# Correction products of a three-product projection on bfloat16 operands instead of float32r

## The chip, the cores and the metric

The kernel runs on one core of a Trainium2 chip. The metric is the device time of one execution, in microseconds (us); the median of the runs shown counts. TensorE (PE) multiplies; PEld is its loading of the stationary operand (the weights of a matmul); VectorE (DVE), ScalarE (ACT) and GpSimd (POOL) work on tiles elementwise; SyncE (SP) issues the DMAs.

## The reference

A decoder trunk of two layers on 1024 tokens of width 1024, in float32. Cut to what matters:

```
for layer in (0, 1):
    h = x @ w_in[layer]                       # [main | mem q | main gate | mem gate]
    y_main = pool(u_main)                     # layer 0: trailing means, windows 2, 4, 8, 16, then a 256x256 map per group
             forgetting_attention(u_main)     # layer 1: 16 heads of 64, keys/values/forget gates = x @ w_kv_shared
    y_mem = memory_attention(q_mem, mem)      # 4 heads of 128 into 256 memory tokens, mkv = mem @ w_mem_kv
    y = concat(y_main * silu(g_main), y_mem * silu(g_mem)) @ w_out[layer]
    x = layer_norm(alpha * x + y)
```

## The kernel before, in words

**Three products for one.** A float32 operand is split into a high part, its rounding to float32r, and a low part, what is left. A product of two such operands is computed as three matmuls into one PSUM bank: high by high, high by low, low by high. All three take float32r operands. `hi_lo` (lines 138 to 142) makes the parts: ACT rounds (line 141), DVE subtracts (line 142). During layer 1's attention the weights are split by `gp_hi_lo` (lines 144 to 146), both operations on POOL; the flag `low` selects it in `split_w` (line 148).

**Slabs.** `slab` (from line 170) computes 128 output columns of a projection for all 1024 tokens: two weight pieces of 4 x 128 rows (`split_w`: a DMA into a `raw` buffer, then the split into `w` tiles, of which there are six, that is three pairs), two PSUM banks of 512 tokens, and for each of 4 row blocks in a piece the three matmuls one behind the other (line 184). One slab is 48 matmuls of 512 columns. Query, key, value, gate and pooling inputs are all slabs, 62 of them.

**The other users of split operands.** `mem_kv` projects the memory tokens (line 218, 256 columns); `probs` in `mem_attention` and the pooling map use `mm3` (line 168); `v_first` (line 622, 272 columns) computes the first values and the forget logits; `OutProj.products` (line 401) the output projection, 12 matmuls for each of 4 banks and each third of the rows. The attention's own logits (also `mm3`, line 168) use keys and queries whose halves are stacked, two float32r matmuls, and are not touched; probabilities by values (line 796) are f16.

**What sets the order.** At the start the x tiles come one by one (`load_x`), and the first two slabs' matmuls are put in order by a scheduler as their inputs come. In the memory attention and in layer 1's attention (`fox`) TensorE's order is written out: `Fill.pump` takes slab matmuls, counted in columns, between the attention's own. The transposes that turn the normed rows of layer 0 into layer 1's input are popped one at a time (`spread`) between projection matmuls. On POOL, layer 1's attention also needs the causal masks (line 736, one for each head and row block, each waiting for DVE's reading of the block before), and the gate products (lines 823 and 833).

**Buffers.** The x stream has two tiles under tag `A` (high and low, 32 KB a partition each); the weights, memory keys, queries and output rows have a pair of tiles each under their tags.

Of the kernel before, what the change touches and what calls it, by code (L numbers as in the profile page):

```python
# [18 lines left out]
P = 128  # L19
# [6 lines left out]
MH = 4  # L26
# [46 lines left out]
def trunk_kernel(ctx, tc, x, xT, memT, win, wk, wv0, wv, wmk, wmv, wout, poolw, pscale, lng, lnb, bforget, out):  # L73
# [42 lines left out]
    def wt(shape):  # L116
        return sb(list(shape), "w", 6, F32R)
# [4 lines left out]
    def w_slots(tags, where):  # L122

        def tiles(k):
            tag, bufs = tags[k]
            if tag == "w":
                return [[wt([P, NH]) for _ in range(2)] for _ in range(2)]
            if tag == "MK":
                pair = [MK([P, 2, NH]) for _ in range(2)]
            elif tag == "PG":  # L130
                pair = [sb([P, 2, NH], "P", 4, F32R), sb([P, 2, NH], "G", 4, F32R)]
            else:
                pair = [sb([P, 2, NH], tag, bufs, F32R, where) for _ in range(2)]
            return [[t[:, j, :] for j in range(2)] for t in pair]

        return tiles

    def hi_lo(hi, lo, src, pinned=False):

        pin = tc.keep_in_program_order if pinned else lambda ins: ins  # L140
        pin(nc.scalar.copy(hi, src))  # L141
        pin(nc.vector.tensor_tensor(lo, src, hi.bitcast(F32), ALU.subtract))  # L142

    def gp_hi_lo(hi, lo, src):
        nc.gpsimd.tensor_scalar(hi, src, 1.0, 1.0, ALU.mult, ALU.mult)  # L145
        nc.gpsimd.tensor_tensor(lo, src, hi.bitcast(F32), ALU.subtract)  # L146

    def split_w(src_dram, shape):
        r = raw(shape)
        nc.sync.dma_start(r, src_dram)  # L150
        h, l = wt(shape), wt(shape)
        (gp_hi_lo if low[0] else hi_lo)(h, l, r)
        return h, l
# [16 lines left out]
    def slab(pieces_dram, XH, XL, evac, banks=("pj", 2)):  # L170
# [4 lines left out]
        for n, pc in ((0, 0), (1, 0), (0, 1), (1, 1)) if arrived else ((0, 0), (0, 1), (1, 0), (1, 1)):  # L175
# [23 lines left out]
    def mem_kv(l):  # L199

        mh = [T([P, 4, NMEM]) for _ in range(2)]
        ml = [T([P, 4, NMEM]) for _ in range(2)]
        for q in range(4):
            r = raw([P, 2, NMEM])
            nc.sync.dma_start(r, memT[:, 2 * q : 2 * q + 2, :])
            hi_lo(mh[q // 2][:, 2 * (q % 2) : 2 * (q % 2) + 2, :], ml[q // 2][:, 2 * (q % 2) : 2 * (q % 2) + 2, :], r)
        kh, kl = MK([P, MH, NMEM]), MK([P, MH, NMEM])

        def project(w_dram):

            acc = ps([P, NH], "pj", 2)[:, :NMEM]
            for pc in range(2):
                a, b = split_w(w_dram[pc], [P, 4, P])
                for k in range(4):
                    if k % 2:
                        spread()
                    for i, (w, m) in enumerate(((a, mh), (a, ml), (b, mh))):
                        nc.tensor.matmul(  # L218
                            acc, w[:, k, :], m[pc][:, k, :],
                            start=pc == 0 and k == 0 and i == 0, stop=pc == 1 and k == 3 and i == 2,  # L220
                        )
            return acc
# [4 lines left out]
        def keys(h):  # L227
            hi_lo(kh[:, h, :], kl[:, h, :], project(wmk[l, h]))
# [9 lines left out]
        return (kh, kl, v, undo), keys, vals  # L238
# [18 lines left out]
    def transposes(src, n, dst_h, dst_l):  # L257

        def one(g, j):
# [3 lines left out]
            if j == 3:  # L263
                hi_lo(dst_h(g), dst_l(g), banks[g])
# [9 lines left out]
    def gate_units(w_dram, dst, XH, XL):  # L274
        return slab(w_dram, XH, XL, lambda cols, acc: gate(acc, dst[:, cols]))

    def mem_attention(l, XH, XL, kv, qtile, ytile, yd):

        (kh, kl, v, undo), keys, vals = kv
# [4 lines left out]
        for h in range(MH):  # L284
            while turns:
                spread()
            qh, ql = qtile(), qtile()
            run(slab(win[l, 8 + h], XH, XL, lambda cols, acc: hi_lo(qh[:, cols], ql[:, cols], acc)))
            qs.append((qh, ql))
# [5 lines left out]
        for h in range(MH):  # L295
            fill.add(gate_units(win[l, 20 + h], gs[h], XH, XL), SLAB)

        def probs(i):
# [3 lines left out]
            for hp in range(2):  # L302
                lg = ps([P, 2, NMEM], "L", 3)
                for j in range(2):
                    h = 2 * hp + j
                    qh, ql = (t[:, i * P : (i + 1) * P] for t in qs[h])
                    mm3(lg[:, j, :], ((qh, kh[:, h, :]), (qh, kl[:, h, :]), (ql, kh[:, h, :])))
# [46 lines left out]
    class OutProj:  # L354
# [23 lines left out]
        def split(self, upto, pinned=False):  # L378

            while self.n < upto:  # L380
# [5 lines left out]
                h, lo = self.ws[nh][kk]  # L386
                hi_lo(h[j], lo[j], self.raws.pop(0), pinned)
# [6 lines left out]
        def products(self, accs, c, yh, yl):  # L394
            for a in range(2):
                for nh in range(2):
                    for k in range(4):
                        kt = 4 * c + k
                        wh, wl = (w[kt % 2] for w in self.ws[nh][kt // 2])
                        for i, (y, w) in enumerate(((yh, wh), (yh, wl), (yl, wh))):  # L400
                            nc.tensor.matmul(  # L401
                                accs[a][nh], y[:, k, a * P : (a + 1) * P], w,
                                start=kt == 8 and i == 0, stop=kt == 7 and i == 2,
# [3 lines left out]
        def early(self, y, yh, yl):  # L407
# [4 lines left out]
            for two in (slice(0, 2), slice(2, 4)):  # L412
                hi_lo(yh[:, two, :], yl[:, two, :], y[:, two, :], True)
                yield
            self.accs = self.open()
            yield from self.products(self.accs, 2, yh, yl)

        def rest(self, resid, XH, XL, dst):
# [11 lines left out]
            for sp, c in order + [(sp, c) for sp in range(2, ST // 2) for c in (2, 0, 1)]:  # L430
                if c == 2:
                    accs[sp] = self.open((("T", 2), ("T", 2), ("L", 3), ("O", 1))) if 0 in accs and sp == 1 else self.open()
                src, yh, yl = T([P, 4, 2 * P], F32), T([P, 4, 2 * P]), T([P, 4, 2 * P])
                nc.sync.dma_start(src, self.yd[c, :, :, sp * 2 * P : (sp + 1) * 2 * P])
                hi_lo(yh, yl, src)
                for k, _ in enumerate(self.products(accs[sp], c, yh, yl)):
                    if c != 2 and k % 6 == 5:
                        spread()
                if c == 1:
                    norm(sp, accs.pop(sp), gb, resid, XH, XL, dst)  # L440

    def norm(sp, accs, gb, resid, XH, XL, dst):
        for a in range(2):
# [22 lines left out]
            if XH is not None:  # L466
                transposes(
                    z, KT,
                    lambda g, rows=rows: XH[:, 4 * g : 4 * g + 4, rows],
                    lambda g, rows=rows: XL[:, 4 * g : 4 * g + 4, rows],  # L470
                )


    XH, XL = (sb([P, KT, S], "A", 2, F32R) for _ in range(2))

    def load_x(kt, parts=1):
        r = T(dt=F32)
        for i in range(parts):
            cols = slice(i * S // parts, (i + 1) * S // parts)
            nc.sync.dma_start(r[:, cols], xT[kt, :, cols])  # L480
            hi_lo(XH[:, kt, cols], XL[:, kt, cols], r[:, cols])
# [17 lines left out]
    with tc.tile_pool(name="in0", bufs=1) as in0:  # L499

        def bt():
            return sb([P, S], "B", 8, F32R, in0)

        def pool_group(g):
            w = WINDOWS[g]
            pms = []
            for f in (2 * g, 2 * g + 1):
                u = sb([P, S], "P", 4)
                run(slab(
                    first[f] if g == 0 else win[0, f], XH, XL, lambda cols, acc: nc.scalar.copy(u[:, cols], acc),  # L510
# [12 lines left out]
                ph, pl = T(), T()  # L523
                hi_lo(ph, pl, pm)
                pms.append((ph, pl))
            r = raw([P, 2, 2 * P])
            nc.sync.dma_start(r, poolw[g])
            wh, wl = (MK([P, 2, 2 * P]) for _ in range(2))
            hi_lo(wh, wl, r)
            ys = []  # L530
            for f in (2 * g, 2 * g + 1):
                y = sb([P, S], "Y", 4, F32, in0)
                run(gate_units(win[0, 12 + f], y, XH, XL))
                ys.append(y)
            for d in range(2):
                f = 2 * g + d
                for n in range(2):
                    acc = ps([P, NH], "L", 3)
                    terms = []
                    for ct in range(2):  # L540
                        a, b = wh[:, ct, d * P : (d + 1) * P], wl[:, ct, d * P : (d + 1) * P]
                        ph, pl = (t[:, n * NH : (n + 1) * NH] for t in pms[ct])
                        terms += [(a, ph), (a, pl), (b, ph)]
# [9 lines left out]
        mem_attention(0, XH, XL, kv, bt, lambda: sb([P, S], "Y", 4, F32, in0), y0d[2])  # L553
# [4 lines left out]
        XH1, XL1 = (sb([P, KT, S], "A", 2, F32R) for _ in range(2))  # L558
        out_proj.rest(x, XH1, XL1, x1)


    XH, XL = XH1, XL1
    with tc.tile_pool(name="in1", bufs=1) as in1:

        def xy(shape=(P, S)):
            return sb(list(shape), "B", 10, F32R, in1)
# [416 lines left out]
```

## Time and profile before

| what | us |
|---|---|
| median of 3 runs | 1236.97 (1236.87 to 1237.36) |
| span of the profiled execution | 1235.9 |
| its own time beside the span (median less span) | about 1.1 |
| TensorE busy | 1223.5, 7018 matmuls |
| DVE / ACT / POOL busy | 787.4 / 567.4 / 170.3 |
| layer 0, about | 0 to 475 |
| layer 1 up to its attention | 475 to 650 |
| attention with slabs between | 650 to 1115 |
| output projection, norm | 1115 to 1236 |

The page gives busy time by engine and in 40 slices; the other views used below group instructions by line and form, list them in order of time (merged when neighbours are alike), and give busy time in chosen stretches. A row of the timeline has start, duration, engine, line, operation, output and inputs, and the count; its duration reaches from the first one's start to the last one's end. A row of groups ends with busy time, mean ns of one, and the idle time before with what ended it.

### The profile page before, as it was taken

How to read it: one execution, taken by the hardware profiler on the slowest of the kernel's cores; microseconds unless marked ns; L12 is line 12 of the kernel's file. 1: busy time of each engine (PE TensorE's matmuls, PEld its weight loads, DVE VectorE, ACT ScalarE, POOL GpSimd, SP SyncE). 2: the span in 40 equal slices, each digit the busy share in tenths (PEclk: the TensorE clock that was granted, in tenths of full speed). 3: DMA queues.
4: the chain of work that ended last, by engine and by line, in shares of the span. 5: the costliest groups of instructions: out<-in, count | busy, mean ns of one | idle time of the engine just before them, and what ended most of it. 6: DMA issues, size and time to landing. Idle time of an engine off the chain costs nothing. (4 is left out here: it accounts for less than half of the span.)

```text
span 1235.9 us, 19603 instructions
## 1 busy us (share of the span) xinstructions
PE 1223.5 (99%) x7018; PEld 1025.8 (83%) x7018; DVE 787.4 (64%) x1853; ACT 567.4 (46%) x1241; POOL 170.3 (14%) x276
## 2 busy tenths in 40 slices
PE   9999999999999999999999999999999999999997
PEld 6888888888888888888898888888888888888885
DVE  6444766375744457357635888878877887775644
ACT  5233662242321123246423777767776777762110
POOL 0000000000000000000002343433334333420000
PEclk9999999999999999999999999999999999999999
DMA  6333543242542324234517778868887989985430
GB/s 230 105 101 86 132 116 131 91 120 86 162 161 102 120 97 151 69 103 111 141 50 181 161 163 188 190 171 180 177 196 162 188 189 220 231 233 178 171 102 34
DMA packets 267409, 178.64 MB, mean 145 GB/s; under 512 B 212272, under 2 KB 225712, under 8 KB 267312
## 3 DMA queue, kind: packets, MB, share of 16 engines
q1 hardware_dynamic: 267312, 177.40, 55.4%
q8 instruction: 55, 0.90, 0.3%
q14 instruction: 42, 0.34, 0.1%
HBM read 94.97 MB, written 22.61 MB: 95 GB/s over the span
## 5 line engine op out<-in xcount | busy, mean ns | idle before, releaser
L184 PE MATMUL pj<-A,w 128*128 128x512 f32 x2928 | 704.7, 392 | 0.7 <-ACT A L141 0.5
L184 PEld LDWEIGHTS pj<-A,w 128*128 128x128 f32 x2928 | 541.9, 188 | 110.6 <-ACT A L141 2.0
L142 DVE TENSOR_TENSOR w<-raw,w 128x512 fp32r<-128x512 f32 x106 | 73.1, 691 | 93.5 <-ACT w L141 88.3
L774 DVE SCALAR_TENSOR_TENSOR P<-T,s,P 128x512 f16<-128x512 f32 x192 | 111.5, 613 | 32.9 <-ACT P L773 31.3
L752 ACT ACTIVATE T<-MK,s 128x512 f32<-128x512 f32 x192 | 111.3, 580 | 42.1 <-DVE s L744 21.8
L773 ACT ACTIVATE P<-T,s 128x512 f16<-128x512 f32 x192 | 102.8, 576 | 44.6 <-ACT T L752 18.8
L141 ACT CAST w<-raw 128x512 fp32r<-128x512 f32 x106 | 65.8, 621 | 113.4 <-PE pj L184 69.6
L168 PE MATMUL L<-B,B 128*128 128x512 f32 (+3 forms) x384 | 89.6, 340 | 0.1
L649 POOL MEMSET G<- 128x128 f32 x1 | 0.2, 204 | 609.8 <-DVE V L351 609.8
L168 PEld LDWEIGHTS L<-B,B 128*128 128x128 f32 x384 | 70.7, 188 | 14.5 <-DVE s L744 1.2
L744 DVE CUSTOM_DVE_ANT_0 MK<-L,R 128x512 f32<-128x512 f32 (+3 forms) x128 | 72.6, 567 | 13.8 <-PE L L168 9.4
L142 DVE TENSOR_TENSOR T<-T,T 128x1024 fp32r<-128x1024 f32 x23 | 28.1, 1223 | 67.4 <-PE pj L401 45.1
L146 POOL TENSOR_TENSOR w<-raw,w 128x512 fp32r<-128x512 f32 x54 | 70.0, 1296 | 4.0 <-PE pj L184 0.6
L736 POOL TENSOR_SCALAR_AFFINE_SELECT R<-R 128x128 f32<-128x128 f32 x128 | 41.6, 330 | 195.4 <-DVE s L744 155.8
L141 ACT CAST T<-T 128x1024 fp32r<-128x1024 f32 x23 | 24.2, 1050 | 93.4 <-DMA T<-y0d 49.7
L796 PEld LDWEIGHTS <-V 128*64 128x64 f16 (+1 forms) x1152 | 49.3, 104 | 13.7 <-issue 9.4
L796 PE MATMUL O<-T,V 128*64 128x128 f16 (+1 forms) x1152 | 57.7, 221 | 0.6 <-DMA T<-P 0.4
L218 PE MATMUL pj<-T,w 128*128 128x256 f32 x384 | 49.2, 285 | 0.2 <-DVE w L142 0.2
L218 PEld LDWEIGHTS pj<-T,w 128*128 128x128 f32 x384 | 48.0, 191 | 1.2 <-DVE w L142 0.5
L401 PE MATMUL pj<-B,T 128*128 128x512 f32 x192 | 47.6, 389 | 0.0
L145 POOL TENSOR_SCALAR w<-raw 128x512 fp32r<-128x512 f32 x54 | 34.0, 629 | 94.1 <-PE pj L184 90.1
L313 ACT ACTIVATE P<-L,s 128x256 f32<-128x256 f32 x64 | 29.5, 473 | 29.9 <-DVE s L310 28.2
(208 smaller groups left out, 1600.4 us busy)
## 6 DMA issues: line engine op xcount, KB each, us to landing
raw<-in_win_dram SPq DMA_DIRECT2D x96, 256.0 KB, 2.8
raw<-in_wout_dram SPq DMA_DIRECT2D x40, 256.0 KB, 2.7
B<-B SPq DMA_DIRECT2D x32, 256.0 KB, 4.0
R<-cumd SPq DMA_DIRECT2D x16, 512.0 KB, 4.6
y0d<-Y SPq DMA_DIRECT2D x12, 512.0 KB, 2.7
T<-y0d SPq DMA_DIRECT2D x12, 512.0 KB, 4.3
T<-y1d SPq DMA_DIRECT2D x11, 512.0 KB, 4.5
raw<-in_wmk_dram SPq DMA_DIRECT2D x16, 256.0 KB, 2.7
```

The lines of the kernel that those rows point to most:

```text
L141: pin(nc.scalar.copy(hi, src))
L142: pin(nc.vector.tensor_tensor(lo, src, hi.bitcast(F32), ALU.subtract))
L146: nc.gpsimd.tensor_tensor(lo, src, hi.bitcast(F32), ALU.subtract)
L168: nc.tensor.matmul(acc, a, b, start=i == 0, stop=i == len(terms) - 1)
L184: nc.tensor.matmul(accs[n], a[:, k, :], b[:, kt, n * NH : (n + 1) * NH], start=kt == 0 and i == 0, stop=kt == KT - 1 and i == 2,)
L218: nc.tensor.matmul(acc, w[:, k, :], m[pc][:, k, :], start=pc == 0 and k == 0 and i == 0, stop=pc == 1 and k == 3 and i == 2,)
L401: nc.tensor.matmul(accs[a][nh], y[:, k, a * P : (a + 1) * P], w, start=kt == 8 and i == 0, stop=kt == 7 and i == 2,)
L744: nc.vector.tensor_tensor_reduce(p[:, lo:up], lg, R[:, lo:up], 1.0, top, ALU.add, ALU.min, m[:, n : n + 1])
L752: nc.scalar.activation(e, p[:, lo:up], AF.Exp, bias=top, scale=-1.0, accum_out=sums[:, n, hd % 2, i : i + 1],)
L773: nc.scalar.activation(pair[:, lo:up], e, AF.Copy, scale=r)
L774: nc.vector.scalar_tensor_tensor(pair[:, L + lo : L + up], e, r, pair[:, lo:up], ALU.mult, ALU.subtract)
L796: nc.tensor.matmul(acc[rows, (i % 4) * P : (i % 4) * P + P], v[:, b, 2 * j : 2 * j + (1 if e else 2), :].rearrange("p e d -> p (e d)"), pt ...
```

## The change

Each split operand becomes a `Split`: a float32r high part as before, and a bfloat16 tile that holds two things, the low part (`lo`) and a copy of the operand rounded to bfloat16 (`top`). High by high stays float32r; the other two products take `top` by `lo` and `lo` by `top`. The bfloat16 pair takes the buffer that the float32r low part had, at the same size. The rounded copy is made on POOL, from the source, or from the high part where the source lies in PSUM; so `gp_hi_lo` has three POOL operations and `hi_lo` has one on each of ACT, DVE and POOL. In `slab`, `mem_kv`'s `project` and `OutProj.products` the loop over the three products moves outside the loop over the four row blocks: four high by high, then four and four of the others. `v_first`, `probs` and the pooling map keep the three one behind the other. In `project` the transposes are popped after the second and third product loops instead of after every other row block; in the output projection they are still popped at every sixth matmul. A bfloat16 matmul has a weight load of its own in the instruction stream, a float32r matmul loads its weights itself.

```diff
-    def hi_lo(hi, lo, src, pinned=False):
+    def parts_of(make, shape):
+        return Split(make(shape), make([shape[0], 2] + list(shape[1:]), BF16))
+
+    def three(a, b):
+        return (a.hi, b.hi), (a.top, b.lo), (a.lo, b.top)
+
+    def hi_lo(to, src, pinned=False, top=None):
         pin = tc.keep_in_program_order if pinned else lambda ins: ins
-        pin(nc.scalar.copy(hi, src))
-        pin(nc.vector.tensor_tensor(lo, src, hi.bitcast(F32), ALU.subtract))
+        pin(nc.scalar.copy(to.hi, src))
+        pin(nc.vector.tensor_tensor(to.lo, src, to.hi.bitcast(F32), ALU.subtract))
+        nc.gpsimd.tensor_scalar(to.top, to.hi.bitcast(F32) if top is None else top, 1.0, 1.0, ALU.mult, ALU.mult)

-    def gp_hi_lo(hi, lo, src):
-        nc.gpsimd.tensor_scalar(hi, src, 1.0, 1.0, ALU.mult, ALU.mult)
-        nc.gpsimd.tensor_tensor(lo, src, hi.bitcast(F32), ALU.subtract)
+    def gp_hi_lo(to, src):
+        nc.gpsimd.tensor_scalar(to.hi, src, 1.0, 1.0, ALU.mult, ALU.mult)
+        nc.gpsimd.tensor_tensor(to.lo, src, to.hi.bitcast(F32), ALU.subtract)
+        nc.gpsimd.tensor_scalar(to.top, src, 1.0, 1.0, ALU.mult, ALU.mult)
...
     def slab(pieces_dram, X, evac, banks=("pj", 2)):
...
-            h, l = ws[pc]
-            for k in range(4):
-                kt = pc * 4 + k
-                for i, (a, b) in enumerate(((h, XH), (h, XL), (l, XH))):
+            for i, (a, b) in enumerate(three(ws[pc], X)):
+                for k in range(4):
+                    kt = pc * 4 + k
                     nc.tensor.matmul(
                         accs[n], a[:, k, :], b[:, kt, n * NH : (n + 1) * NH],
...
-        def products(self, accs, c, yh, yl):
+        def products(self, accs, c, ys):
             for a in range(2):
                 for nh in range(2):
-                    for k in range(4):
-                        kt = 4 * c + k
-                        wh, wl = (w[kt % 2] for w in self.ws[nh][kt // 2])
-                        for i, (y, w) in enumerate(((yh, wh), (yh, wl), (yl, wh))):
+                    for i in range(3):
+                        for k in range(4):
+                            kt = 4 * c + k
+                            y, w = three(ys[:, k, a * P : (a + 1) * P], self.ws[nh][kt // 2][kt % 2])[i]
...
         def project(w_dram):
...
-                a, b = split_w(w_dram[pc], [P, 4, P])
-                for k in range(4):
-                    if k % 2:
-                        spread()
-                    for i, (w, m) in enumerate(((a, mh), (a, ml), (b, mh))):
+                for i, (w, m) in enumerate(three(split_w(w_dram[pc], [P, 4, P]), ms[pc])):
+                    for k in range(4):
...
+                    if i:
+                        spread()
```

The rest of the diff hands the `Split` objects through where pairs of tiles were handed before.

More of the change, by code (lines that the diff above doesn't have):

```diff
@@ L150, in split_w @@
         nc.sync.dma_start(r, src_dram)
-        h, l = wt(shape), wt(shape)
-        (gp_hi_lo if low[0] else hi_lo)(h, l, r)
-        return h, l
+        to = parts_of(wt, shape)
+        if low[0]:
+            gp_hi_lo(to, r)
+        else:
+            hi_lo(to, r, top=r)
+        return to
     ident = const.tile([P, P], F32, name="ident")
@@ L465, in norm, with stream @@
                 nc.sync.dma_start(dst[rows, cols], z[:, cols])
[L466 to L474, printed above, removed]
+            if X is not None:
+                transposes(z, KT, lambda g, rows=rows: X[:, 4 * g : 4 * g + 4, rows])
+    def stream(shape, dt=F32R):
+        return sb(shape, "A", 2, dt)
+    X = parts_of(stream, [P, KT, S])
     def load_x(kt, parts=1):
@@ L885, in fox @@
                         if step == 9:
[L886 removed]
+                            lead = out_proj.early(land((P, 4, 2 * P)), parts_of(xy, (P, 4, 2 * P)))
                             next(lead)
```

143 lines of the change are left out of this document (71 added, 72 removed).

## The prediction

> **What bounds the kernel now.** I read the page first, for shares and slices.
>
> ```profile
> span 1235.9 us, 19603 instructions
> PE 1223.5 (99%) x7018; PEld 1025.8 (83%) x7018; DVE 787.4 (64%) x1853; ACT 567.4 (46%) x1241; POOL 170.3 (14%) x276
> PE   9999999999999999999999999999999999999997
> POOL 0000000000000000000002343433334333420000
> ```
>
> TensorE is busy in every slice, and only it: whatever shortens its queue of matmuls shortens the kernel, until another engine comes late. POOL, which gets new work, is empty outside the attention stage. The busy time by stretch says how near the others are:
>
> ```profile
> 650.00:1115.00 465.00, 464.19 (x3017) 383.82 (x3016) 363.30 (x1026) 320.30 (x731) 168.00 (x268) 1.00 0.85 190
> ```
>
> (Columns: PE, PEld, DVE, ACT, POOL.) Between 650 and 1115 us DVE is at 78%, ACT at 69%, POOL at 36%, TensorE at 99.8%. So the price of one matmul, start to start, decides. "Busy" does not give that, because matmuls overlap; the timeline does: a group of n lasts n-1 steps and the last one's own duration, which the groups by form give.
>
> ```profile
> 204.69 17.61 PE L184 MATMUL pj<-A,w 128*128 128x512 f32 x77
> 1.25 4.02 PE L92 MATMUL idle<-warm 128*128 128x512 bf16 x9 [1.25 <-DVE warm L89]
> 101.47 1.72 PE L218 MATMUL pj<-T,w 128*128 128x256 f32 x13
> 187.18 2.84 PE L168 MATMUL T<-T,MK 128*128 128x128 f16 x48
> ...
> L184 PE MATMUL pj<-A,w 128*128 128x512 f32 x2928 | 704.7, 392 | 0.7 <-ACT A L141 0.5
> L218 PE MATMUL pj<-T,w 128*128 128x256 f32 x384 | 49.2, 285 | 0.2 <-DVE w L142 0.2
> L92 PE MATMUL idle<-warm 128*128 128x512 bf16 x9 | 4.0, 631 | 1.3 <-DVE warm L89 1.3
> L168 PE MATMUL T<-T,MK 128*128 128x128 f16 x288 | 17.6, 219 | 0.5 <-DMA T<-P 0.5
> L168 PEld LDWEIGHTS <-MK 128*128 128x128 f16 x384 | 21.5, 98 | 1.2 <-issue 1.1
> ```
>
> float32r, 512 columns: (17.61 - 0.39)/76 = 226.6 ns. 256 columns: (1.72 - 0.285)/12 = 119.6 ns. The two give 107 ns per 256 columns and a fixed part of 12.6 ns. f16, 128 columns, with a new weight load each: (2.84 - 0.219)/47 = 55.8 ns. At 107 ns per 256 columns its streaming is 53.5, so its fixed part is 2.3 ns although each load lasts 98 ns: loads of 16-bit weights hide completely, and the fixed part is about 10.5 ns less than for float32r.
>
> **The change part by part.** *Two of three products become bfloat16.* In the built program the number of matmuls is unchanged; of them 2816 with 512 columns (1984 in the slabs, 768 in the output projections, 64 in the pool mixing), 384 with 256 and 128 with 272 are now bfloat16 with a weight load of their own. The trace has bfloat16 matmuls of 512 columns only among the first nine, at (4.02 - 0.63)/8 = 424 ns, where every step still takes about twice its later time; none at this speed. Bounds: the f16 fixed part (214 + 2.3 = 216 ns, the nearest row for 16-bit operands) and no gain (227 ns). I take the f16 row: it measures the same kind of load in front of each matmul. Then 3328 x 10.5 ns = **-35 us**; at the other bound 0.
>
> *Switches.* The new loops put four float32r products, then eight bfloat16 ones, in a row, and the attention's float32r logits and the 32-bit transposes cut into these runs. Counted in the built order, TensorE goes 656 times from float32r to 16-bit operands and 656 times back; before, 36 times each. So 620 new ones in each direction. The trace has both, at the memory values:
>
> ```profile
> 183.81 0.84 PE L184 MATMUL pj<-A,w 128*128 128x512 f32 x3
> 184.49 0.29 PE L168 MATMUL T<-T,MK 128*128 128x128 f16 x2
> ...
> 189.53 0.50 PE L168 MATMUL T<-T,MK 128*128 128x128 f16 x6
> 189.83 0.70 PE L184 MATMUL pj<-A,w 128*128 128x512 f32 x2
> ...
> 189.81 0.53 PEld L184 LDWEIGHTS pj<-A,w 128*128 128x128 f32 x3
> ```
>
> Into 16 bit: the last float32r starts at 183.81 + 0.84 - 0.39 = 184.26, the second f16 at 184.49 + 0.29 - 0.22 = 184.56; 300 ns where 227 + 56 = 283 would be clean. That is about 15 ns (rounding: 5 to 25), and 620 x 15 = **+9 us** (+3 to +16). Back: the last f16 starts at 189.53 + 0.50 - 0.22 = 189.81, the second float32r at 189.83 + 0.70 - 0.39 = 190.14; 330 to 340 ns, so 50 to 57 ns more than clean. Is that the price of the type, or of a short matmul that cannot cover the next load? The float32r load starts at 189.81, at once with the last f16 matmul, so it is not held back. And float32r behind short float32r:
>
> ```profile
> 1085.79 0.39 PE L184 MATMUL pj<-A,w 128*128 128x512 f32 x1
> 1086.01 0.40 PE L168 MATMUL L<-B,B 128*128 128x256 f32 x2
> 1086.24 0.86 PE L184 MATMUL pj<-A,w 128*128 128x512 f32 x3
> ...
> 1088.99 0.39 PE L184 MATMUL pj<-A,w 128*128 128x512 f32 x1
> 1089.22 0.33 PE L168 MATMUL L<-B,B 128*128 128x128 f32 x2
> 1089.39 0.68 PE L184 MATMUL pj<-A,w 128*128 128x512 f32 x2
> ```
>
> With two of 256 columns between, the third float32r after them starts at 1086.24 + 0.86 - 0.39 = 1086.71, 0.92 after 1085.79; clean is 3 x 0.227 + 2 x 0.120 = 0.92: nothing lost. With two of 128 columns, 1089.68 - 1088.99 = 0.69, clean 2 x 0.227 + 2 x 0.060 = 0.57: 50 to 60 ns lost for each short one, without any change of type. So length sets it. In the new order the way back follows 512 columns, or 256 to 272 in 165 cases. I take **0**; the other end is 57 ns each, +35 us, a rival below.
>
> *Short ones in front of a 16-bit load.* 40 transposes or 128-column logits now have a bfloat16 product behind them instead of a float32r one: the 57 ns go (the 15 are counted above), 40 x 57 = **-2 us**.
>
> The Trainium skill ("TensorE: Matmul & The Clock Gate", Part 3, The mechanism) says that a weight load overlaps matmuls in flight only when the row groups differ, which speaks against this change, since all loads here use the whole array; the 55.8 ns step against 98 ns loads of the same shape does not agree.
>
> *Start.* Here the order matters: before, each x tile opens three products for each of four banks; now only the high one until all four tiles of a half have arrived.
>
> ```profile
> 0.00:11.60 11.60, 9.73 (x24) 5.39 (x25) 5.73 (x24) 6.91 (x9) 0.70 (x6) 1.00 0.79 291
> ...
> 10.53 1.06 ACT L141 CAST A<-T 128x1024 fp32r<-128x1024 f32 x1 [0.21 <-DMA T<-in_xT_dram]
> 16.52 2.95 ACT L141 CAST A<-T 128x1024 fp32r<-128x1024 f32 x3
> ...
> 30.07 10.14 PE L184 MATMUL pj<-A,w 128*128 128x512 f32 x44
> ```
>
> Until 11.6 us, when the fourth tile is rounded (10.53 + 1.06), 24 - 9 warming matmuls = 15 products ran; the new order has 12 that can. Three times 0.227 is 0.7 us. Then 22 more follow without a wait, to about 16.4, and the next needs the sixth tile, rounded at 16.52 + 2.95/3 = 17.5: 1.1 us. Together **+1.8 us**; bounds 0 and 4 (a second such wait, or the slow steps of the first microseconds, 424 ns, lasting longer because of the gaps).
>
> *Other engines.* DVE writes the low part as bfloat16 instead of float32r, same count. POOL gets 236 roundings and a third operation in each of its 54 weight splits (and ACT nothing new).
>
> ```profile
> L146 POOL TENSOR_TENSOR w<-raw,w 128x512 fp32r<-128x512 f32 x54 | 70.0, 1296 | 4.0 <-PE pj L184 0.6
> L145 POOL TENSOR_SCALAR w<-raw 128x512 fp32r<-128x512 f32 x54 | 34.0, 629 | 94.1 <-PE pj L184 90.1
> L142 DVE TENSOR_TENSOR w<-raw,w 128x512 fp32r<-128x512 f32 x106 | 73.1, 691 | 93.5 <-ACT w L141 88.3 <-PE pj L401 4.3
>   POOL R L736: 4.4, 4
> ```
>
> Outside attention the 0.63 us of a rounding runs beside ACT's and DVE's work on the same piece (0.69 for the low part), so it is ready no later: 0. In attention POOL gets 54 x 0.63 = 34 us and some roundings for the output weights, 48% instead of 36%. What waits behind it in its queue are the masks (line 736), for which DVE waited only 4.4 us, 4 times (last row: who ended DVE's idle time at line 744), and the last gate products before the output projection. The weights themselves are split a slab's half ahead, at least 24 matmuls or 5 us against 1.9 + 0.63. I take 0, other end +5. Queues of SP and the bytes moved are unchanged: buffers keep their sizes, the bfloat16 pair filling the place of the old low part.
>
> *The sum*: -35 + 9 + 0 - 2 + 1.8 + 0 = -26 us. Against the profiled execution's 1235.9 us that is 1210; what lies around the span is 1.1 us (median 1237.0), so **1211 us**. Nothing else is late next: DVE at 363 of 455 us would still be at 80%.
>
> **The rivals.** (1) *Each way back costs 57 ns* whatever its cover, because the type and not the length sets it: -26 + 35 = +9, **1246 us**. It decides from 26/620 = 42 ns. For: the f16 rows; against: the rows of 128 and 256 columns. (2) *POOL becomes the bound in attention*: if each of the 128 masks stood behind one more rounding and DVE waited for it, 128 x 0.63 = 80 us; a quarter of that gives back 20 of the 26: **1231 us**. For: POOL serves in order; against: 4.4 us of waits now. (3) *No gain in the matmul*: 512 bfloat16 columns step like float32r; only switches and start remain, **1246 us**. Against: the f16 step. (4) *Loads do not hide*: 98 ns more on each of 3328, +326 - 26: **1537 us**. Against: 55.8 ns again; this is what the overlap rule of the Trainium skill, cited above, would do here. (5) *More gain*: in the attention stage steps behind short matmuls are a little long; the products after 1089.39 are an example, and if bfloat16 ones are immune, some 6 us more: **1204 us**.
>
> **How the numbers follow.** Forecast 1211 us: chance 0.6. Rival 5: 0.13. Rival 2 and partial forms of rival 1 (a few ns to 25 ns per switch), which land between 1216 and 1234: 0.1. Rival 1 in full or worse: 0.1. Rival 3: 0.05. Rival 4: 0.02. The range takes the switch into 16 bit at 3 to 16 us, start and POOL at their ends, rival 5 and the partial forms: 1198 to 1232. A measurement of this kernel tells about 0.2% from no change. Faster 0.8, same 0.04, slower 0.16.
>
> **What would show it.** In the profile of the changed kernel: groups of bfloat16 matmuls at 216 ns a step; the first float32r behind them at 216 to 230 after the last bfloat16 one (rival 1: 270 or more); about 15 ns at the way in; POOL at some 48% between 650 and 1095, with DVE's waits for the masks still a few us; the third slab, which now starts at 30.07 (last row of the start's lines), starting some 1.3 us later, the new products' own gain taken off; TensorE still at 98 to 99%. The prediction is wrong if TensorE shows idle time in attention, or if a block of 12 products takes over 2.72 us.

## The result, and the profile after

| | median us | runs | ratio to before |
|---|---|---|---|
| before | 1237.03 (1236.87 to 1237.36) | 4 | |
| after | 1229.59 (1228.54 to 1231.2) | 4 | 0.9944 [0.993, 0.9959] |

Faster by 7.4 us, where 26 were forecast. The same lines of the page as before, for the changed kernel, and the stretch of the attention stage (PE, PEld, DVE, ACT, POOL):

```profile
span 1228.6 us, 20280 instructions
PE 1202.2 (98%) x7018; PEld 731.9 (60%) x7018; DVE 839.8 (68%) x1853; ACT 567.3 (46%) x1241; POOL 415.8 (34%) x582
PE   8999999999999999999999999999999999999997
POOL 7233102151421225320203454544445434573110
```

```profile
650.00:1115.00 465.00, 459.76 (x3031) 291.04 (x3029) 364.89 (x1012) 318.84 (x730) 221.24 (x349) 1.00 0.83 188
```

Read the first two lines against those of before. TensorE's busy time fell by 1223.5 - 1202.2 = 21.3 us, but the span less the busy time grew from 1235.9 - 1223.5 = 12.4 to 1228.6 - 1202.2 = 26.4, by 14.0. So two things are to be explained: why the matmuls gave 21 and not 28 (the forecast's -35 + 9 - 2), and why TensorE stands 14 us longer and not 1.8. By stage, 3.7 of the 14 lie before the third slab, 4.5 from there to the first values of layer 1's attention, 3.2 in the attention and 2.6 behind it. POOL is at 221.24/465 = 48% in the attention stage, as forecast. DVE is the surprise: 787.4 to 839.8 us busy with the same 1853 instructions. The groups by form say which ones, and the list of DVE's waits says whom it now waits for (us in total, times, longest):

```profile
L160 DVE TENSOR_TENSOR w<-raw,w 128x512 bf16<-128x512 f32 x106 | 101.5, 960 | 60.7 <-PE pj L206 43.3 <-ACT w L159 11.4 <-POOL w L161 4.2
L160 DVE TENSOR_TENSOR T<-T,T 128x1024 bf16<-128x1024 f32 x23 | 34.2, 1487 | 43.2 <-PE pj L420 24.3 <-ACT T L159 16.0 <-POOL T L161 2.9
L160 DVE TENSOR_TENSOR B<-pj,B 128x512 bf16<-128x512 f32 x16 | 11.0, 684 | 24.9 <-ACT B L159 24.9
L161 POOL TENSOR_SCALAR w<-raw 128x512 bf16<-128x512 f32 x106 | 75.3, 712 | 255.5 <-PE pj L206 163.7 <-issue 26.6 <-DVE s L328 17.3
```

```profile
DVE w L160 <- POOL w L161: 4.2, 2, 3.0
DVE T L160 <- POOL T L161: 4.1, 2, 2.9
DVE MK L756 <- POOL R L748: 4.0, 4, 1.9
```

The subtraction that makes a low part (line 160; line 142 before) takes 960 ns where it took 691, and 1487 on 1024 columns where it took 1223. Its output became smaller, so the type is hardly why; the run with the rounding on ACT, below, has the same types and 699 ns. DVE's waits for POOL's roundings (4.2 and 4.1 us) are new and short; the subtraction itself is longer. Of the 106 subtractions `w<-raw,w`, the 16 that have POOL at work beside them for less than a twentieth of their time take 680 ns on average, the 26 that have it for more than four fifths take 1051. The 47 that have it for about half take 1080: some 537 ns of them are without POOL and the rest beside its rounding, as if the two took turns. The third row is the contrast: the same operation with its source in PSUM (`pj`), all 16 with POOL beside them for more than four fifths, takes 684. The masks (third wait) are waited for as before: 4.0 us, 4 times.

How the matmuls now step is read from the weight loads, whose rows keep the two types apart, and from short windows of the timeline:

```profile
205.27 1.41 PEld L206 LDWEIGHTS <-w 128*128 128x128 bf16 x8 [0.28 <-issue]
...
207.94 1.41 PEld L206 LDWEIGHTS <-w 128*128 128x128 bf16 x8 [0.27 <-issue]
...
210.61 1.41 PEld L206 LDWEIGHTS <-w 128*128 128x128 bf16 x8 [0.28 <-issue]
```

```profile
205.50 1.46 PE L206 MATMUL pj<-A,w 128*128 128x512 bf16 x6
```

```profile
207.71 0.40 PE L206 MATMUL pj<-A,w 128*128 128x512 f32 x1
```

```profile
208.17 0.38 PE L206 MATMUL pj<-A,w 128*128 128x512 bf16 x1
```

A bfloat16 step is (1.46 - 0.38)/5 = 0.216 us, exactly the f16 row's figure that the forecast took. A block of 12 (8 bfloat16, 4 float32r) takes 207.94 - 205.27 = 2.67 and again 210.61 - 207.94 = 2.67. All float32r it would be 12 x 0.2267 = 2.72, so a block wins 50 ns; eight steps 10.7 ns shorter, less the forecast's 15 for one switch, would win 71. From the last float32r start (207.71) to the second bfloat16 start (208.17) are 0.46 to 0.47 where 0.227 + 0.216 = 0.443 is clean: 22 ns for the way in.

The theory to be tested (A): POOL's new roundings and DVE's subtraction keep each other from SBUF, the parts come late, TensorE waits; a smaller part is lost to switches at about 33 ns a pair, and to the new order at the start. Rivals: (B) TensorE waits for the rounded copies themselves; (C) the idle time comes from the new order of the loops alone; (D) switches cost nothing, and the steps are long for another reason.

### The profile page after: what moved, and what is told of

It reads as the page before. It is cut to its first block, busy times and chain, and to the rows that moved or that the text cites. A ratio compares the mean times of both kernels' runs of the same rounds, so it can differ in the third digit from the quotient of the medians.

```text
span 1228.6 us, 20280 instructions
## 1 busy us (share of the span) xinstructions
PE 1202.2 (98%) x7018; PEld 731.9 (60%) x7018; DVE 839.8 (68%) x1853; ACT 567.3 (46%) x1241; POOL 415.8 (34%) x582
## 5 line engine op out<-in xcount | busy, mean ns | idle before, releaser
L206 PE MATMUL pj<-A,w 128*128 128x512 bf16 (+1 forms) x2928 | 691.8, 399 | 7.1 <-DVE A L160 2.0
L206 PEld LDWEIGHTS <-w 128*128 128x128 bf16 x1984 | 170.3, 98 | 236.1 <-issue 65.8
L206 PEld LDWEIGHTS pj<-A,w 128*128 128x128 f32 x976 | 179.2, 189 | 56.1 <-ACT A L159 3.9
L161 POOL TENSOR_SCALAR w<-raw 128x512 bf16<-128x512 f32 x106 | 75.3, 712 | 255.5 <-PE pj L206 163.7
L160 DVE TENSOR_TENSOR w<-raw,w 128x512 bf16<-128x512 f32 x106 | 101.5, 960 | 60.7 <-PE pj L206 43.3
L420 PEld LDWEIGHTS <-T 128*128 128x128 bf16 x736 | 64.6, 98 | 88.2 <-issue 24.2
L165 POOL TENSOR_TENSOR w<-raw,w 128x512 bf16<-128x512 f32 x54 | 69.7, 1292 | 25.4 <-PE pj L206 25.1
L160 DVE TENSOR_TENSOR T<-T,T 128x1024 bf16<-128x1024 f32 x23 | 34.2, 1487 | 43.2 <-PE pj L420 24.3
L420 PE MATMUL pj<-B,T 128*128 128x512 bf16 (+1 forms) x192 | 54.4, 399 | 0.0
L420 PE MATMUL L<-B,T 128*128 128x512 f32 (+1 forms) x168 | 48.0, 405 | 1.2 <-POOL T L161 1.2
```

Source lines behind the costliest of these rows:

```text
L160: pin(nc.vector.tensor_tensor(to.lo, src, to.hi.bitcast(F32), ALU.subtract))
L161: nc.gpsimd.tensor_scalar(to.top, to.hi.bitcast(F32) if top is None else top, 1.0, 1.0, ALU.mult, ALU.mult)
L165: nc.gpsimd.tensor_tensor(to.lo, src, to.hi.bitcast(F32), ALU.subtract)
L206: nc.tensor.matmul(accs[n], a[:, k, :], b[:, kt, n * NH : (n + 1) * NH], start=kt == 0 and i == 0, stop=kt == KT - 1 and i == 2,)
L420: nc.tensor.matmul(accs[a][nh], y, w, start=kt == 8 and i == 0, stop=kt == 7 and i == 2,)
```

## The experiments

All ratios are to the kernel before, run on the same chip in the same job (1235.58, 1236.35 and 1236.3 us in the three jobs).

**The order alone.** The kernel before, all float32r, with only the loops exchanged:

```diff
-            for k in range(4):
-                kt = pc * 4 + k
-                for i, (a, b) in enumerate(((h, XH), (h, XL), (l, XH))):
+            for i, (a, b) in enumerate(((h, XH), (h, XL), (l, XH))):
+                for k in range(4):
+                    kt = pc * 4 + k
```

> The kernel before with the new loop order alone: all three products stay float32r, four of each kind in a row. Theory A (TensorE's new 12 us of idle time come from POOL's roundings slowing DVE's subtractions): only the start changes, +1 to +3 us, 1238 to 1240 us, and TensorE's idle time rises by that alone. Rival C (the idle time comes from the order, since a group of four needs all its inputs at once): most of the 12 us show here, 1245 to 1249 us.

Measured: 1238.92 us, 1.0021 [1.0012, 1.0031], as expected of theory A. In the profiles all of it comes at the start: the third slab begins at 32.85 instead of 30.07 us, no later stage is longer by as much as 0.5 us, and one is 1.4 shorter. Windows between 5 and 15 us, of the kernel before and then of this one:

```profile
5.00:10.00 5.00, 4.39 (x10) 2.93 (x10) 2.92 (x4) 3.31 (x5) 0.00 (x0) 1.00 1.00 387
10.00:15.00 5.00, 5.00 (x23) 4.07 (x22) 4.26 (x5) 2.95 (x4) 0.00 (x0) 1.00 1.04 422
```

```profile
5.00:10.00 5.00, 3.40 (x6) 1.55 (x6) 2.57 (x4) 2.74 (x5) 0.00 (x0) 1.00 1.03 397
10.00:15.00 5.00, 5.00 (x15) 3.84 (x15) 4.26 (x5) 3.30 (x4) 0.00 (x0) 1.00 1.03 417
```

Only 6 matmuls lie between 5 and 10 us instead of 10, and 15 between 10 and 15 instead of 23: the new order has less to run until a half of x has arrived, and the long steps of the beginning last longer. A product starts every 427 ns until 14.0 us here and until 10.3 us in the kernel before; half of those 3.7 us, 1.9, is an estimate of what that costs. So the order costs 2.8 us (forecast 1.8). TensorE's span less its busy time rises by only 1.1 us, from 12.4 to 13.5, and rival C falls as the cause of the rest.

**The rounding on ACT.** The changed kernel with the copy made by the engine that makes the high part:

```diff
-        nc.gpsimd.tensor_scalar(to.top, to.hi.bitcast(F32) if top is None else top, 1.0, 1.0, ALU.mult, ALU.mult)
+        pin(nc.scalar.copy(to.top, src))
```

> The changed kernel with the rounded copy of hi_lo made on ACT instead of POOL (the attention's weight splits stay on POOL). Theory A: DVE's subtraction on 128x512 falls back from 960 to about 690 ns, and the kernel gains 6 to 11 us against the changed one, 1219 to 1224 us; a part may be lost to ACT being later by 0.6 us at each split. Rival B (TensorE waits for the copies themselves, whoever makes them): no gain, about 1230 us or more, since ACT makes two copies one after the other.

Measured: 1224.06 us, 0.9904 [0.9889, 0.9919], 5 us better than the change (6 to 11 were expected), although ACT has 140 us more to do. DVE's subtraction, same 106:

```profile
L160 DVE TENSOR_TENSOR w<-raw,w 128x512 bf16<-128x512 f32 x106 | 74.1, 699 | 80.5 <-PE pj L206 50.8 <-ACT w L159 22.4 <-PE pj L236 3.3
```

Back at 699 ns. That is POOL's presence, but not yet its price.

**No rounding, and a rounding that nobody reads.** The upper half of a float32r number is a bfloat16 number, so the copy can be read in place, with a step of two, cut off instead of rounded. The next kernel does that and drops the rounding; the one after keeps the rounding on POOL, into a tile that nothing reads (the last line of the diff is its own; `upper` takes every second element of the tile seen as bfloat16):

```diff
-            self.hi, self.lo, self.top = hi, pair[:, 0], pair[:, 1]
+            self.hi, self.lo, self.top = hi, pair[:, 0], upper(hi)
...
-        nc.gpsimd.tensor_scalar(to.top, to.hi.bitcast(F32) if top is None else top, 1.0, 1.0, ALU.mult, ALU.mult)
+        nc.gpsimd.tensor_scalar(to.spare, to.hi.bitcast(F32) if top is None else top, 1.0, 1.0, ALU.mult, ALU.mult)
```

> The changed kernel without any rounding of copies: top is the upper 16 bits of the float32r high part, read in place with a step of two (cut off instead of rounded, so the correction products are slightly different). Theory A and rival B alike: the idle time goes back to about 5 us, DVE's subtraction to 690 ns, 1216 to 1221 us. Rival C: still about 1229 us. If a bfloat16 operand with a step of two is read more slowly, its matmuls take more than 216 ns a step and the time is above 1230 us.

> As e4_top_in_place, but POOL still makes every rounded copy, into the place it has in the changed kernel, and nobody reads it. Theory A (POOL's work slows DVE, whose low parts come late): about as the changed kernel, 1226 to 1230 us, with DVE's subtraction at 950 ns. Rival B (TensorE waits for the copies): as e4_top_in_place, 1216 to 1221 us.

Measured: 1230.15 us, 0.9955 [0.994, 0.9969], and 1240.42 us, 1.004 [1.0028, 1.0053]; both are some 10 us above what theory A expected (1216 to 1221 and 1226 to 1230). The subtraction without, then with the spare rounding, and POOL's row of the latter:

```profile
L167 DVE TENSOR_TENSOR w<-raw,w 128x512 bf16<-128x512 f32 x106 | 73.4, 694 | 87.2 <-PE pj L211 57.9 <-ACT w L166 28.3 <-issue 0.5
```

```profile
L167 DVE TENSOR_TENSOR w<-raw,w 128x512 bf16<-128x512 f32 x106 | 99.7, 942 | 69.6 <-PE pj L213 47.5 <-ACT w L166 15.1 <-POOL w L168 3.1
L168 POOL TENSOR_SCALAR w<-raw 128x512 bf16<-128x512 f32 x106 | 76.4, 722 | 256.3 <-PE pj L213 183.2 <-DVE s L336 17.2 <-DMA raw<-in_win_dram 13.2
```

Nothing waits for the spare copies except what stands behind them on POOL, and they still cost (1.004 - 0.9955) x 1235.6 = 10.5 us. TensorE's waits that DVE ended, the first one at the warming matmuls left out, come to 1.4 us without them and to 5.2 us with them. Rival B falls as the main cause: it is less the copy that is late than what DVE makes beside it. (In the changed kernel TensorE does stand 1.2 us, once, for a copy itself.)

The kernel without any rounding was still no faster than the change. Its blocks show what lengthened both kernels; here the bfloat16 products with the stationary operand in place, then those with the moving operand in place, then the loads:

```profile
207.33 0.81 PE L211 MATMUL pj<-A,w 128*128 128x512 bf16 x3
```

```profile
207.97 0.84 PE L211 MATMUL pj<-A,w 128*128 128x512 bf16 x3
```

```profile
205.95 0.88 PEld L211 LDWEIGHTS pj<-A,w 128*128 128x128 f32 x4
...
208.66 0.88 PEld L211 LDWEIGHTS pj<-A,w 128*128 128x128 f32 x4
```

(0.81 - 0.38)/2 = 0.216 against (0.84 - 0.39)/2 = 0.226: a bfloat16 moving operand read with a step of two goes at float32r's step, a stationary one does not. The block takes 2.71 us, hardly less than 2.72.

**Does POOL's reading matter, or its presence?** The kernel with the spare roundings, each replaced by two fills of the same tile:

```diff
-        nc.gpsimd.tensor_scalar(to.spare, to.hi.bitcast(F32) if top is None else top, 1.0, 1.0, ALU.mult, ALU.mult)
+        nc.gpsimd.memset(to.spare, 0.0)
+        nc.gpsimd.memset(to.spare, 0.0)
```

> The kernel with the spare roundings (copies read in place, cut off instead of rounded; POOL still writes a copy that nobody reads), but with each spare rounding replaced by two fills of the same tile with a constant: POOL writes SBUF as often, and reads nothing. Theory A (DVE's subtraction and POOL's rounding shut each other out because both read SBUF, the subtraction with two inputs): the subtraction is back near 690 ns and the time at that of the kernel with the copies in place and no rounding, ratio 0.9955. Rival (any POOL instruction that uses SBUF beside the subtraction delays it): subtraction 900 ns or more wherever a fill lies beside it, ratio 1.00 to 1.004.

Measured: 1232.51 us, 0.997 [0.9958, 0.9982]. Page, and the groups of DVE and POOL:

```profile
PE 1207.4 (98%) x6914; PEld 729.7 (59%) x7018; DVE 787.7 (64%) x1853; ACT 567.6 (46%) x1241; POOL 497.0 (40%) x888
```

```profile
L167 DVE TENSOR_TENSOR w<-raw,w 128x512 bf16<-128x512 f32 x106 | 73.1, 690 | 86.1 <-PE pj L215 60.6 <-ACT w L166 22.1 <-ACT P L347 1.7
```

```profile
L168 POOL MEMSET w<- 128x512 bf16 x106 | 55.6, 524 | 322.1 <-PE pj L215 295.0 <-PE pj L245 18.3 <-PE pj L429 6.7
```

POOL is busier than ever (497 us), 87 of the 106 subtractions have it beside them for more than four fifths of their time, and they take 691 ns; DVE's busy time, 787.7 us, is that of the kernel before. (This trace lacks some matmul records: 6914 of 7018.) So the two shut each other out only if both read: POOL's instruction must read SBUF, and DVE's must read two operands there. In time, the fills give back (1.004 - 0.997) x 1236.3 = 8.7 of the 10.5 us, and TensorE's waits that DVE ended are at 1.6 us. A longer queue on POOL is thus hardly what the roundings cost. The fills differ in one thing more, they do not hold the piece's `raw` buffer; but what the DMAs into those buffers waited for most is DVE's subtraction, 209 us in all with the spare roundings, 169 without and 167 with the fills.

The Trainium skill ("SBUF — State Buffer", Who interferes with whom) says that a DVE instruction with two SBUF inputs contends with a GpSimd instruction that reads SBUF, and not with one that only writes it; it calls the shared ports an exclusive lock. The runs agree with that rule: 680 and 1051 ns, 684 with one input in PSUM, 691 beside fills.

**Fewer and more switches.** First every second group is reversed, so that groups of one type meet (505 switches each way for 656); then the loops go back to the old order, with bfloat16 operands (1604). Both are done in the slabs, shown here, and in the output projection:

```diff
-            for i, (a, b) in enumerate(three(ws[pc], X)):
+            for i, (a, b) in list(enumerate(three(ws[pc], X)))[:: 1 - 2 * pc]:
```

```diff
-            for i, (a, b) in enumerate(three(ws[pc], X)):
-                for k in range(4):
-                    kt = pc * 4 + k
+            for k in range(4):
+                kt = pc * 4 + k
+                for i, (a, b) in enumerate(three(ws[pc], X)):
```

> The changed kernel (ratio 0.9944 to the kernel before) with the order of every second group of 12 reversed, so that groups of one type meet: 151 fewer ways from float32r into 16 bit and 151 fewer back (505 instead of 656 each); nothing else changes. Theory A (a pair of switches costs some 33 ns, from the profile after: about 22 on the way in, 5 on the way back, and a few ns more on the float32r steps between): 151 x 33 = -5 us against the changed kernel, ratio about 0.990. Theory B (switches cost nothing; the 12 products take 2.67 us because the float32r steps of the changed kernel are longer for another reason): no change, ratio 0.9944.

> The changed kernel with the loops of the slabs and of the output projection in the order of the kernel before (each weight tile's three products together): 1604 switches each way instead of 656, 948 more. Theory A (33 ns a pair): +31 us, less about 2.8 for the start, which goes back to the old order, and less if DVE's waits are hidden behind the longer steps: ratio 1.012 to 1.018. Theory B (switches cost nothing): 0.992. The price as the prediction had it, 15 ns on the way in and 0 back: +14 - 3 = +11 us, ratio 1.003.

Measured: 1232.17 us, 0.9964 [0.9952, 0.9977], no gain at all, and 1240.28 us, 1.0033 [1.0021, 1.0044], so 1.0033 - 0.9944 = 0.9%, 11 us for 948 pairs, where theory A expected some 28. Neither came out by theory A as written. The weight loads tell what a switch does to the steps, first with fewer, then with more:

```profile
206.74 1.79 PEld L206 LDWEIGHTS pj<-A,w 128*128 128x128 f32 x8
208.79 3.14 PEld L206 LDWEIGHTS <-w 128*128 128x128 bf16 x16 [0.27 <-issue]
212.04 1.09 PEld L206 LDWEIGHTS pj<-A,w 128*128 128x128 f32 x5
```

```profile
204.71 0.12 PEld L206 LDWEIGHTS <-w 128*128 128x128 bf16 x2 [0.26 <-issue]
...
209.45 0.11 PEld L206 LDWEIGHTS <-w 128*128 128x128 bf16 x2 [0.25 <-issue]
```

A block of 8 + 16 takes 212.04 - 206.74 = 5.30 us (median of all such blocks 5.307); two of 4 + 8 take 5.34. With 1 + 2 seven blocks take 209.45 - 204.71 = 4.74, 0.677 to 0.680 each: what three float32r products take, 3 x 0.2267 = 0.680. Against clean steps (226.7 and 216 ns) a pair of switches costs 5.307 - (8 x 0.2267 + 16 x 0.216) = 0.037 us in runs of 8 + 16, 2.670 - (4 x 0.2267 + 8 x 0.216) = 0.035 in runs of 4 + 8, and 0.680 - (0.2267 + 2 x 0.216) = 0.021 in runs of 1 + 2. So there is a price, and rival D falls; but the longer float32r runs pay more, because their steps do not come back to 226.7: in the trace of the changed kernel the medians within a run of four are 230 and 231 ns, then 239 before the bfloat16 ones. Why they do not is open.

Then why did fewer switches win nothing? Its start is worse (windows between 5 and 15 us; the third slab begins at 35.44 us, at 33.83 in the change), and so is a stretch of attention; TensorE's waits there are listed last:

```profile
5.00:10.00 5.00, 1.96 (x5) 0.75 (x4) 2.46 (x3) 2.35 (x4) 3.00 (x4) 0.87 1.00 381
10.00:15.00 5.00, 4.92 (x12) 3.20 (x13) 4.91 (x3) 2.64 (x4) 4.79 (x4) 0.50 1.03 419
...
990.00:1040.00 50.00, 47.48 (x327) 32.43 (x329) 40.53 (x115) 36.32 (x86) 19.88 (x33) 0.97 0.93 206
```

```profile
PE O L810 <- DMA T<-P: 3.5, 3, 2.1
```

Attention (first value product to second output projection) takes 398.07 us instead of 394.91 and the start 1.6 more; all the rest together is 2.9 shorter, near the 151 x 21 to 33 ns = 3 to 5 expected. So the switches' gain is there in the other stages, and waits and a lower clock took it back. The waits are among others those for the transposed probabilities that come by DMA (3.5 us in three waits, the longest 2.1; in the changed kernel 1.9). The clock stands at 0.50 from 8.8 to 15.6 us, in the changed kernel from 9.8 to 13.2, and again from 1005.4 to 1008.9 us, where the changed kernel keeps 1.00; each of these 3.4 us more is worth about 1.7 us (half of it, an estimate). That is not the whole: two executions of this kernel with a mean clock of 0.997 and 0.998 took 1231.2 and 1231.5 us, the profiled one, with 0.993, 1232.4. What made that DMA late was not tried.

**Dense moving copies on ACT, stationary ones in place.** This puts together what the runs above showed: no POOL rounding, and a step of two only where it is free:

```diff
+            self.top = pair[:, 1] if moving else upper(hi)
...
-        nc.gpsimd.tensor_scalar(to.top, to.hi.bitcast(F32) if top is None else top, 1.0, 1.0, ALU.mult, ALU.mult)
+        if to.moving:
+            pin(nc.scalar.copy(to.top, src))
```

> The changed kernel with no rounding on POOL: a stationary operand's copy is the upper 16 bits of its high part, read in place with a step of two (cut off instead of rounded, so its correction products differ slightly), and a moving operand's copy is made dense, by ACT. Theory A: the contention of POOL with DVE's subtraction is gone, as in the run with all copies in place, and the 16-bit products with a moving operand of step two, which took 227 ns there instead of 216, are at 216 again: 1230 - 1408 x 10.5 ns = 1215 us, ratio 0.983 (0.980 to 0.987). Rival: the step of 227 ns there did not come from the moving operand's step of two, but from the reading of a float32r tile; then the time is that of the run with the rounding on ACT at best, ratio 0.990 or more.

Measured: 1222.49 us, 0.9882 [0.9867, 0.9897]; against the kernel with all copies in place 0.9955 - 0.9882 = 0.7%, 9 us, not 15. The steps did as theory A said; here the three products with the copy as moving operand, and the loads:

```profile
206.94 0.81 PE L214 MATMUL pj<-A,w 128*128 128x512 bf16 x3
```

```profile
206.06 1.41 PEld L214 LDWEIGHTS <-w 128*128 128x128 bf16 x8 [0.27 <-issue]
...
208.74 1.41 PEld L214 LDWEIGHTS <-w 128*128 128x128 bf16 x8 [0.28 <-issue]
```

(0.81 - 0.38)/2 = 0.216, and the block at 2.68 instead of 2.71. By their medians the blocks win 36 ns (2.707 and 2.671 us) and not the 4 x 10.5 = 42 that the expectation counted: the step from the last float32r product to the first bfloat16 one is 239 ns here and 230 there. For 352 blocks that makes 13 us of its 15, if all were whole; but in runs of one and two the step behind a switch is 227 ns either way. What the rest is was not followed up.

**With the old order at the start, and fewer switches.** The last kernel, with the first two slabs in the order of the kernel before and every second group reversed elsewhere:

```diff
+            if arrived:
+                todo = [(i, k) for k in range(4) for i in range(3)]
+            else:
+                todo = [(i, k) for i in ((2, 1, 0) if pc else (0, 1, 2)) for k in range(4)]
```

> The one before this (moving copies by ACT, stationary ones in place and cut off) with the first two slabs in the loop order of the kernel before, so that products start with each x tile, and every second group of 12 reversed elsewhere (521 switches each way). Theory A: 2.8 us less at the start, less what the switches there cost, and 135 pairs of switches x 33 ns = 4.5 us less: some 6 us below the one before this, ratio about 0.978 (0.974 to 0.984). Theory B (switches cost nothing, start as predicted): 2 us below, ratio 0.981 if the one before this is at 0.983.

Measured: 1214.21 us, 0.9823 [0.981, 0.9837]: 1.2% below the change, 1.8% below the kernel before. The start:

```profile
5.00:10.00 5.00, 4.03 (x14) 1.83 (x13) 2.84 (x4) 4.04 (x7) 0.00 (x0) 1.00 1.04 404
10.00:15.00 5.00, 5.00 (x24) 2.31 (x24) 3.42 (x4) 5.00 (x7) 0.00 (x0) 1.00 1.04 421
```

14 and 24 matmuls lie there, 6 and 15 in the order-alone kernel; the third slab begins at 28.68 us, 3.8 before that of the kernel with stationary copies in place. A good part of this is the clock: in that kernel products start every 427 ns or more from 9.5 to 14.1 us, and here the steps are mostly 215 to 240 ns from 5.8 us on wherever TensorE has its inputs. The other stages are 4.9 us shorter together: 135 pairs fewer x 35 ns = 4.7. So this time the switches' gain reached the end. That fits POOL being out of DVE's way; but the start was changed with it, so the runs do not show that one by itself.

## Why the prediction was wrong, point by point

**"Other engines ... I take 0, other end +5"** is the step that failed. It put POOL's 0.63 us "beside ACT's and DVE's work on the same piece", as if engines that run side by side did not slow each other, and bounded POOL by its queue alone. The spare roundings show 10.5 us for it, twice its other end; moved to ACT, the roundings gave 5 us back. (It also counted 236 roundings; the trace has 252 of them, line 161, beside the 54 third operations.) The trace of before could not show the price, since POOL was nearly empty outside attention, but the rule of the Trainium skill cited above says beforehand which of DVE's instructions would pay: those with two operands in SBUF, and a subtraction of a rounded tile from its source in SBUF is one. The concern for the queue was mistaken: POOL came to the 48% forecast, and the masks were waited for 4.0 us, 4.4 before. Rival 2 gave 1231 us, close to the result, but by luck: its reason was the masks, which the trace refutes.

**-35 us for the matmuls**: right. The bfloat16 step is 216 ns; rivals 3 and 4 (no gain; loads that do not hide) are out.

**+9 for the ways in, 0 for the ways back**: too small. 15 ns was read from an f16 row of 128 columns; a pair costs 35 in the blocks of 4 + 8 and 21 in runs of 1 + 2. Some 300 of the 620 ways in follow a run of four or more float32r products of 512 columns: 300 x 35 + 320 x 21 = 17 us, an estimate, 8 more than forecast. The way back by itself is small, as forecast (rival 1's 57 ns is refuted); the start of the first float32r behind a bfloat16 run is moved, not its successor:

```profile
206.82 1.04 PE L206 MATMUL pj<-A,w 128*128 128x512 f32 x3
```

The last bfloat16 product starts at 205.50 + 1.46 - 0.38 + 0.216 = 206.80, the third of these float32r at 206.82 + 1.04 - 0.39 = 207.47: 0.67 to 0.68 us where 0.216 + 2 x 0.227 = 0.67 is clean.

**-2 for the short ones**: mostly not there. From a 512-column product over a 32-bit transpose and one more product to the next took 573 ns as a median before (48 places) and takes 541 (25 places) with bfloat16 neighbours; clean is 227 + 60 + 227 = 514 and 216 + 60 + 216 = 492, so the loss is 59 and 49 ns. With the 21 ns of the pair of switches around the transpose taken off, 28 are left: of the 57 ns that were to go, 10 to 31 went, 0.4 to 1.2 us in all at the forecast's 40 places.

**+1.8 for the start**: the wait for a half of x is right, the size is 2.8 by the order alone, and 3.8 in the changed kernel (33.83 less 30.07), where the roundings come on top. The sum took 0.227 us a product, where TensorE stepped at 427 ns until 10.3 us; that these slow steps would last longer, to 14.0 us with the order alone, stood only in its upper bound of 4.

**The two tests named at the end.** A block takes 2.67 us, below the 2.72 set. Idle time in the attention stage did appear: 465 - 464.19 = 0.8 us became 465 - 459.76 = 5.2.

Summed up, in the profiles: the matmuls gave 21.3 us and not 28, and TensorE stands 14.0 us longer and not 1.8. Some 17 us for the switches instead of 9 and about 1 for the short ones instead of 2 give -35 + 17 - 1 = -19 for the matmuls, so some 2 us came from elsewhere. Rival 5, slow steps in attention, can be a part of it at most: by the same prices, busy time fell by 2.0 us more than the sum in the attention, but also by 2.8 more between the first output projection and the attention. Of the 14 us the order makes 1.1 by itself. TensorE's waits that DVE ended, the first one left out again, rose from 0.2 to 7.4 us, and with the rounding on ACT they are 2.9. The rest, some 6 us, are mainly waits that ACT and DMAs ended, and no run separates them. In time, the roundings' price is 5 us by the run with ACT, which had copies of its own to make, and 10.5 with the copies in place. A sum that closes was not measured.

## What to carry to other kernels

Work given to an idle engine is not free because it lies beside other work: look at what its neighbours read, and take their durations where they overlap, not the quiet ones. Price a change of operand type by the length of the runs between the changes, from a block of the very mix. And a saving in the bounding engine counts only in those stages where its inputs were early; where another engine has just become slower, expect to lose part of it again.

## What the runs showed of the hardware

- A bfloat16 moving operand with a step of two goes at float32r's 226 to 227 ns for 512 columns, dense at 216; a stationary one with a step of two costs nothing. So the 11 ns seem to belong to the moving operand's spacing in memory, not to the weight load.
- POOL's fills beside DVE's two-input subtraction cost it nothing (691 ns), POOL's roundings half its duration again (1051 for 680).
- The granted clock can fall where TensorE waits at the start. The changed kernel's windows (clock: third column from the right):

```profile
5.00:10.00 5.00, 2.77 (x7) 1.29 (x7) 3.10 (x4) 2.72 (x5) 3.46 (x5) 0.98 0.96 345
10.00:15.00 5.00, 4.83 (x16) 2.60 (x15) 4.88 (x4) 3.01 (x5) 5.00 (x4) 0.68 1.04 419
```

Within the second window the clock is at 0.50 until 13.2 us, where products start every 427 ns, and at 1.00 behind it, with steps of 215 and 216 ns. In the five other profiles with 1.96 to 3.22 us busy between 5 and 10 us it reads 0.50 to 0.73 between 10 and 15; in the last kernel (4.03) and the one with more switches (3.33) it stays at 1.00. A thin stretch at the start was thus followed by half speed in six of the eleven profiles, and so paid twice. The column alone can mislead: in the other three it reads 1.00 where the steps are still 427 ns (until 10.3 us in the kernel before, 14.0 with the order alone, 13.6 with the spare roundings), so the steps are to be looked at too. The Trainium skill ("TensorE: Matmul & The Clock Gate", Part 1, What's actually happening) describes the clock as two states, half and full, chosen by recent activity; 0.50 and 1.00 agree, and 0.68 is a mean over both.
